# A hybrid decoder step on one core: the samples' value rows go to all partitions by DMA through scratch memory, not by products with a selecting matrix

## The chip, the cores and the metric

The kernel runs on one core of a Trainium2 chip. A core has a matrix engine (TensorE, PE in the rows), VectorE (DVE), ScalarE (ACT), GpSimd (POOL) and SyncE (SP), and 16 DMA engines that serve transfers issued from SP and from GpSimd. The metric is the device time of one execution, in microseconds (us), as the median of several runs.

## The reference

A two-layer decoder trunk is computed for 256 prompt tokens and for 8 samples of one new token each. Layer 0 mixes by pooling, layer 1 by gated linear attention (GLA); each is followed by an MLP, and all four blocks by a layer norm. The change lies in the state update of the GLA layer for the samples. Cut to that:

```python
q, k, v, og, gk_low = jnp.split(x @ w_in, ...)          # 4 heads, DK = 256, DV = 512
log_a = log_sigmoid(gk_low @ w_gate_up + gate_bias) / 16
# per token: S_t = diag(a_t) S_{t-1} + k_t^T v_t ;  o_t = q_t S_t
S_new = S * exp(b_last) + einsum('bhjk,bhjv->bhkv', k, v)
o = einsum('bhik,bhkv->bhiv', q * exp(bcum), S) + ...
```

For a sample there is one token, so for each sample and head the 256 x 512 state is scaled row by row by `a`, the outer product of the sample's key (256 numbers) and value row (512 numbers) is added, the new state is written out, and it is multiplied with the query.

## The kernel before

**Layout.** Activations lie transposed: features on the 128 partitions, and 264 columns (256 prompt tokens, then the 8 samples). Weights are read in units of 128 x 2048. `stage()` issues a unit's load from SP and splits each half in two parts, `whi` (a cast on ScalarE, L134) and `wlo` (a subtraction on VectorE, L135); `project()` makes 16 x 3 products of a unit (L147 to L149) into a bank `ps`. Six halves, three units, are held, and a unit is staged two units ahead of its use.

**Order.** TensorE's program is in the order in which the code is written; the other engines' programs are ordered by a scheduler. `project()` calls `slot()` after every 12 products. A `slot()` runs what `later()` has put off, and moves each background chain on to its next `yield`. So one `yield` in a chain is a slot of 12 products, and all side work of GLA stands between such slots. The chains are `main_chain` (prompt attention, head after head), `sample_chain` (the samples, head after head) and `rms_chain`.

**Values.** `Head.value(t, ...)` is called for each of the four 128-feature tiles of a head's values. Some slots later its `turn()` transposes the tile on TensorE against `ident` into a bank `ma` (there are two such banks): two transposes for the prompt (L509, copied by L513 to `vtok`), and a third for the samples (L510, from `vp`, the samples' 8 columns as two parts, copied by L514 to `vs`).

**Samples.** `Head.samples()` handles 8 samples in two rounds of four. `load(b)` brings both halves of a sample's state from memory on SP's queue into `s0`, which has nine buffers for the eight halves of a round; `decay(b)` scales it on ScalarE (L612). Per sample, TensorE multiplies `vs` by a column of `pick` that is repeated 128 times; this leaves the sample's 512-value row on all partitions of the bank `mc` (L629). VectorE then adds key times row to each half of the state (L632), and GpSimd issues its store (L633). Two more yields and the next sample follows; after four of them come eight products of states and queries (L643). Buffers of `s0` come free when these products and the stores have read them. At the end of a head the result is transposed (L657).

**Prompt.** In `Head.chain()` the score products of a level (L474) are copied from `ma` under a mask (L478); after the attention products (L528) the keys are turned (L565) and copied to `ktok` (L566), and two slots or so later the new prompt state is made from it (L572) and stored by GpSimd (L575).

Of the kernel before, what the change touches and what calls it, by code (L numbers as in the profile page):

```python
# [6 lines left out]
F32 = mybir.dt.float32  # L7
F32R = mybir.dt.float32r
U8 = mybir.dt.uint8
AF = mybir.ActivationFunctionType  # L10
ALU = mybir.AluOpType
PSUM = bass.MemoryType.PSUM

P = 128
D = 2048
KT = D // P
NP = 256
NS = 8
# [7 lines left out]
DV = 512  # L26
# [20 lines left out]
def hybrid_step(tc, a, o, stop=None):  # L47
    nc = tc.nc
    with ExitStack() as ctx, tc.manual_schedule(engines={mybir.EngineType.PE}):
        _body(ctx, tc, nc, a, o, stop)  # L50


def _body(ctx, tc, nc, a, o, stop):
    V, S, PE, G = nc.vector, nc.scalar, nc.tensor, nc.gpsimd
# [5 lines left out]
    work = pool("work", 6)  # L60
# [3 lines left out]
    def wtile():  # L64
        return work.tile([P, N], F32, name="wt")

    def bank(tag):
        return misc.tile([P, 512], F32, name=tag, bufs=2 if tag == "ma" else 1)
# [3 lines left out]
    ident = keep.tile([P, P], F32, name="ident")  # L72
# [11 lines left out]
    def hslot(s, i, shape, dt, name):  # L84
        return hp.tile(shape, dt, name=name, tag=f"{s}{i}")
# [78 lines left out]
    def later(n, fn):  # L164
        pending.append([n, fn])

    def project(x, ncol=N):
        w = next_unit()
        ps = acc.tile([P, NX], F32, name="ps")
        for k in range(KT):  # L170
            c = slice((k % 8) * P, (k % 8 + 1) * P)
            hi, lo = w[k // 8]
            mm3(ps[:, :ncol], hi[:, c], lo[:, c], x.hi[k][:, :ncol], x.lo[k][:, :ncol], k == 0, k == KT - 1)
            if k % 4 == 3:
                slot()
        return ps
# [186 lines left out]
    def gla(gctx, norm, xp, x, hg):  # L363
        gp = gctx.enter_context(tc.tile_pool(name="gp", bufs=1))
# [21 lines left out]
        wg = gp.tile([P, KT * 32], F32, name="wg", tag="st", bufs=2)  # L386
        low = gp.tile([P, N], F32, name="low", tag="st", bufs=2)
        nc.sync.dma_start(wg, a["wgk"])
        pick = gp.tile([P, NS], F32R, name="pick")
        G.memset(pick.bitcast(F32), 0.0)  # L390
        G.tensor_tensor(pick[:2 * NS], ident[:2 * NS, :NS], ident[:2 * NS, NS:2 * NS], op=ALU.add)

# [34 lines left out]
        class Head:  # L429
# [64 lines left out]
            def value(self, t, ps, raw):  # L494
                v = wtile()
                evacuate(v, ps, raw)

                vp = work.tile([P, 2 * NS], F32R, name="vp", bufs=4)
                V.tensor_copy(vp[:, :NS], v[:, NP:])
                V.tensor_tensor(vp[:, NS:], v[:, NP:], vp[:, :NS].bitcast(F32), op=ALU.subtract)  # L500

                def turn():
                    if t == 0:
                        self.vtok = [hslot(hg, 8 + 2 * self.h + b, [P, DV], F32, "vtok") for b in range(2)]
                        self.vs = hslot(hg, self.h % 2, [P, DV], F32R, "vs")
                        V.memset(self.vs.bitcast(F32), 0.0)
                    tp = bank("ma")
                    for b in range(2):
                        PE.transpose(tp[:, b * P:b * P + P], v[:, b * P:b * P + P], ident)  # L509
                    PE.transpose(tp[:2 * NS, NP:NP + P], vp.bitcast(F32), ident)  # L510
                    c = slice(t * P, t * P + P)
                    for b in range(2):
                        V.tensor_copy(self.vtok[b][:, c], tp[:, b * P:b * P + P])  # L513
                    S.copy(self.vs[:2 * NS, c], tp[:2 * NS, NP:NP + P])  # L514
                    self.turned = t + 1

                if not raw:
                    later(2, turn)
                else:
                    self.turns = getattr(self, "turns", []) + [turn]  # L520
                    if t == 3:
                        for e, fn in enumerate(self.turns):
                            later(2 + e, fn)
# [77 lines left out]
            def samples(self):  # L601
                h = self.h
                s0s = {}

                def load(b):
                    s0s[b] = [half("s0") for _ in range(2)]
                    for hf in range(2):
                        nc.sync.dma_start(s0s[b][hf], a["st"][h, b][:, hf])

                def decay(b):  # L610
                    for hf in range(2):
                        S.mul(s0s[b][hf], s0s[b][hf], sa[:, 2 * h + hf, b:b + 1])  # L612

                for b in range(4):
                    load(b)
                while self.turned < 4:
                    yield
                for r in range(2):
                    V.tensor_copy(qpad[:, :, 4 * r:4 * r + 4, r], self.q[:, :, NP + 4 * r:NP + 4 * r + 4])
                decay(0)  # L620
                yield
                op = bank("mb")
                for r in range(2):
                    if r:
                        decay(4)
                        yield
                    for b in range(4 * r, 4 * r + 4):
                        vb = bank("mc")
                        PE.matmul(vb, lhsT=pick[:, b:b + 1].broadcast_to([P, P]), rhs=self.vs, start=True, stop=True)  # L629
                        for hf in range(2):  # L630
                            s0 = s0s[b][hf]
                            V.scalar_tensor_tensor(s0, vb, self.k[:, hf, NP + b:NP + b + 1], s0, ALU.mult, ALU.add)  # L632
                            nc.gpsimd.dma_start(o["ngs"][h, b][:, hf], s0)  # L633
                        yield
                        if b % 4 < 3:
                            decay(b + 1)
                            yield
                            yield
                    yield
                    for hf in range(2):  # L640
                        for c in range(4):
                            b = 4 * r + c
                            PE.matmul(op[32 * c:32 * c + 32], lhsT=qpad[:, hf, b], rhs=s0s[b][hf],  # L643
                                      start=r == 0 and hf == 0, stop=r == 1 and hf == 1, tile_position=(0, 32 * c))
                        yield
                    if r == 0:
                        for b in range(4, NS):
                            load(b)
                        yield
                        yield  # L650
                os_ = gp.tile([P, DV], F32, name="os", tag="st", bufs=2)
                S.copy(os_, op)
                yield
                yield
                tp = bank("ma")
                for t in range(4):
                    PE.transpose(tp[:, t * P:t * P + P], os_[:, t * P:t * P + P], ident)  # L657
                tv = tp.rearrange("p (t c r) -> p t r c", t=4, c=4)
                V.tensor_copy(self.oT[:, :, NP:].rearrange("p t (r c) -> p t r c", r=2), tv[:, :, :2])
                self.sampled = True  # L660
# [32 lines left out]
        def evacuate(dst, ps, raw, scale=1.0):  # L693
            if raw:
                t, col = settle(ps)
                V.tensor_scalar(dst, t, col, scale, ALU.subtract, ALU.mult)
            else:
                S.mul(dst, ps[:, :N], scale)

        heads = []  # L700
        gated = Parts(hg, ())
# [39 lines left out]
    with tc.tile_pool(name="poolp", bufs=2) as pp:  # L741
# [68 lines left out]
        ln = Norm("mix_0", xs, 0, half=True, first=4)  # L810
# [20 lines left out]
    ln = mlp(0, ln, xs, Parts("b"), lambda: Parts("a"))  # L831
# [2 lines left out]

    with ExitStack() as gctx:
        xr = Parts("b")
        gated = gla(gctx, ln, ln.x, xr, "a")
        for m in range(KT):
            S.mul(Z[m], xr.hi[m][:, :N].bitcast(F32), ALPHA)
            V.scalar_tensor_tensor(Z[m], xr.lo[m][:, :N].bitcast(F32), ALPHA, Z[m], ALU.mult, ALU.add)  # L840
        xs = Parts("b")
        tc.keep_in_program_order(S.preload_act_table(AF.Abs_reciprocal_sqrt))
        ln = Norm("mix_1", xs)
        for m in range(KT):
            ln.add(project(gated))
    if stop == "gla":
        return dump(ln)
    ln = mlp(1, ln, xs, Parts("a"), None)
# [94 lines left out]
```

## Time and profile before

| what | value |
|---|---|
| median of 3 runs | 2057.54 us (2055.9 to 2058.04) |
| the profiled execution's own time | 2056.8 us |
| its span from first to last instruction | 2055.0 us |
| granted TensorE clock, mean | 0.993 of full |
| TensorE busy | 2022.8 us, 98% of the span |
| VectorE, ScalarE, GpSimd busy | 61%, 52%, 3% |

The span is 1.8 us shorter than the execution's own time. Matmuls are pipelined, so each shows a duration that overlaps the next one's; what a matmul costs is read from start to start. GpSimd's row for a transfer is the time it takes to issue it, and "to landing" is from issue until the data have arrived. GLA's side work lies between about 866 and 1170 us.

### The profile page before, as it was taken

The numbers are of one execution on the slowest core, as the hardware profiler recorded it, in microseconds if no ns is written. First come the engines' busy times: TensorE is split into PE (matmuls) and PEld (weight loads), VectorE is DVE, ScalarE is ACT, GpSimd is POOL, SyncE is SP. The second block draws the span as 40 slices with busy tenths as digits, with TensorE's granted clock in tenths as the row PEclk, the third lists the DMA queues.
The fourth block names the chain that finished last, engine by engine and source line by source line (L and its number), as shares of the span: only waits on it lengthen the run. The fifth ranks groups of instructions, "written<-read, shape, count | busy, mean of one in ns | idle before, by whom it ended". The sixth has DMA issues, their size and how long they took to land.

```text
span 2055.0 us, 38509 instructions
## 1 busy us (share of the span) xinstructions
PE 2022.8 (98%) x16308; PEld 1985.2 (97%) x16308; DVE 1255.5 (61%) x1983; ACT 1077.8 (52%) x1618; POOL 54.8 (3%) x129
## 2 busy tenths in 40 slices
PE   8899999999999999999999999999999999999996
PEld 7899999999999999998899999999999999999996
DVE  6866455444444568986778768866445444445465
ACT  4457355345435545856666645566454345435543
POOL 0000000000000000011111010000000000000000
PEclk9999999999999999999999999999999999999998
DMA  7555555555555554477676455545555555555552
GB/s 293 182 183 185 185 180 178 178 184 184 185 175 177 182 185 168 160 257 258 244 264 235 165 177 174 180 170 183 185 185 182 178 176 183 185 181 179 178 180 84
DMA packets 66877, 387.76 MB, mean 189 GB/s; under 512 B 7856, under 2 KB 10672, under 8 KB 25216
## 3 DMA queue, kind: packets, MB, share of 16 engines
q1 hardware_dynamic: 60816, 366.01, 51.3%
q0 software_dynamic: 5888, 19.30, 2.5%
q8 instruction: 127, 2.08, 0.4%
q14 instruction: 46, 0.38, 0.1%
HBM read 364.24 MB, written 22.14 MB: 188 GB/s over the span
## 4 chain that ended last, share of the span: by engine, by line
PE 94%; DVE 4%; DMA 1%; ACT 1%; issue 0%; SPq 0%; ACTq 0%; POOL 0%; DVEq 0%
PE ps L147 30%; PE ps L148 30%; PE ps L149 30%; PE ma L474 1%; PE mb L643 1%; PE ma L572 1%; DVE wlo L135 1%; PE ps L792 0%; PE mc L629 0%; DMA pw<-in_pw 0%; DVE zt L302 0%; PE ma L528 0%; DMA s<-in_st 0%; DVE zt L303 0%; DMA raw<-in_w 0%
## 5 line engine op out<-in xcount | busy, mean ns | idle before, releaser
L148 PE MATMUL ps<-hl,whi 128*128 128x264 f32 (+1 forms) x5120 | 1455.7, 284 | 0.0
L147 PE MATMUL ps<-hh,whi 128*128 128x264 f32 (+1 forms) x5056 | 1449.4, 287 | 4.5 <-ACT whi L134 4.5
L149 PE MATMUL ps<-hh,wlo 128*128 128x264 f32 (+1 forms) x5056 | 1436.1, 284 | 3.4 <-DVE wlo L135 3.4
L135 DVE TENSOR_TENSOR wlo<-raw,whi 128x1024 fp32r<-128x1024 f32 x640 | 783.6, 1225 | 594.8 <-ACT whi L134 592.2
L134 ACT CAST whi<-raw 128x1024 fp32r<-128x1024 f32 x640 | 671.4, 1051 | 840.6 <-PE ps L148 806.0
L147 PEld LDWEIGHTS ps<-hh,whi 128*128 128x128 f32 x5056 | 952.7, 188 | 21.3 <-issue 15.8
L148 PEld LDWEIGHTS ps<-hl,whi 128*128 128x128 f32 x5120 | 965.2, 189 | 3.7 <-issue 1.4
L149 PEld LDWEIGHTS ps<-hh,wlo 128*128 128x128 f32 x5056 | 952.8, 188 | 3.7 <-DVE wlo L135 3.7
L180 DVE TENSOR_TENSOR hl<-wt,hh 128x264 fp32r<-128x264 f32 x188 | 80.0, 432 | 17.6 <-ACT hh L179 11.7
L179 ACT CAST hh<-wt 128x264 fp32r<-128x264 f32 x188 | 76.9, 412 | 7.5 <-DVE wt L666 3.3
L355 DVE TENSOR_TENSOR zt<-zt,ps 128x264 f32<-128x264 f32 x96 | 41.2, 429 | 61.6 <-PE ps L149 61.5
L341 ACT ACTIVATE wt<-wt 128x264 f32<-128x264 f32 x128 | 54.6, 427 | 4.0
L632 DVE SCALAR_TENSOR_TENSOR s<-mc,k,s 128x512 f32<-128x512 f32 x64 | 45.8, 746 | 3.0 <-PE mc L629 3.0
L340 ACT ACTIVATE wt<-ps,par 128x264 f32<-128x264 f32 x96 | 45.7, 476 | 0.0
L612 ACT ACTIVATE s<-s,sa 128x512 f32<-128x512 f32 x64 | 43.0, 718 | 3.4 <-DMA s<-in_st 3.3
L633 POOL DMA_DIRECT2D out_ngs<-s x64 | 34.7, 542 | 348.3 <-DVE s L632 340.5
L213 DVE SCALAR_TENSOR_TENSOR zt<-ps,zt 128x264 f32<-128x264 f32 x48 | 20.8, 434 | 35.5 <-PE ps L149 35.5
L792 PE MATMUL ps<-px,pw 128*128 128x264 f32 x128 | 31.9, 403 | 3.7 <-DMA pw<-in_pw 3.7
L255 ACT ACTIVATE wt<-zt 128x264 f32<-128x264 f32 x60 | 23.7, 412 | 16.8 <-DVE zt L213 16.7
L792 PEld LDWEIGHTS ps<-px,pw 128*128 128x128 f32 x128 | 24.7, 199 | 8.1 <-issue 3.8
L248 ACT ACTIVATE hh<-zt,par 128x264 fp32r<-128x264 f32 x48 | 24.4, 512 | 12.5 <-DVE zt L213 8.8
L304 ACT ACTIVATE wt<-zt,par 128x264 f32<-128x264 f32 x48 | 27.6, 604 | 1.1 <-DVE zt L303 1.1
(178 smaller groups left out, 851.7 us busy)
## 6 DMA issues: line engine op xcount, KB each, us to landing
raw<-in_w SPq DMA_DIRECT2D x256, 1024.0 KB, 4.8
raw<-in_win SPq DMA_DIRECT2D x48, 1024.0 KB, 5.3
s<-in_st SPq DMA_DIRECT2D x64, 256.0 KB, 5.6
out_ngs<-s POOLq DMA_DIRECT2D x64, 256.0 KB, 3.2
raw<-in_wout SPq DMA_DIRECT2D x16, 1024.0 KB, 4.8
pw<-in_pw SPq DMA_DIRECT2D x4, 1024.0 KB, 8.8
zt<-in_xf SPq DMA_DIRECT2D x4, 528.0 KB, 9.4
out_y<-zt SPq DMA_DIRECT2D x8, 264.0 KB, 2.2
```

What stands on the lines that cost most here:

```text
L134: S.copy(hi, src)
L135: V.tensor_tensor(lo, src, hi.bitcast(F32), op=ALU.subtract)
L147: PE.matmul(ps, lhsT=whi, rhs=xh, start=start, stop=False)
L148: PE.matmul(ps, lhsT=whi, rhs=xl, start=False, stop=False)
L149: PE.matmul(ps, lhsT=wlo, rhs=xh, start=False, stop=stop_)
L179: S.copy(x.hi[m][:, :N], src)
L180: V.tensor_tensor(x.lo[m][:, :N], src, x.hi[m][:, :N].bitcast(F32), op=ALU.subtract)
L340: S.activation(t, project(x)[:, :N], AF.Relu, bias=bias)
L341: S.activation(t, t, AF.Square)
L612: S.mul(s0s[b][hf], s0s[b][hf], sa[:, 2 * h + hf, b:b + 1])
L632: V.scalar_tensor_tensor(s0, vb, self.k[:, hf, NP + b:NP + b + 1], s0, ALU.mult, ALU.add)
L792: PE.matmul(ps[:, :N], lhsT=w[:, c], rhs=px[2 * g + k // 2][:, k % 2], start=k == 0, stop=k == 3)
```

## The change

The three-part transposing and the products with `pick` go. The samples' columns of the four value tiles are gathered in one tile `vp`; after the fourth turn a single transpose makes 32 rows of 128 from it, ScalarE copies them to `vs`, and GpSimd stores them to a scratch tensor `vd` in device memory, ordered by sample. For each sample `spread(b)` then reads its 512-value row from there, repeated for all 128 partitions, into `vb`, which has two buffers (`hslot` 0 and 1). The first two spreads are issued at the head's start; each further one is issued when both halves of the sample two before it have been updated, and ahead of that sample's two stores. The head's first update comes two slots later than it did. GpSimd's program, in GLA only, is in source order.

```diff
-        pick = gp.tile([P, NS], F32R, name="pick")
-        G.memset(pick.bitcast(F32), 0.0)
-        G.tensor_tensor(pick[:2 * NS], ident[:2 * NS, :NS], ident[:2 * NS, NS:2 * NS], op=ALU.add)
+        dram = gctx.enter_context(tc.tile_pool(name="dram", bufs=2, space=bass.MemoryType.DRAM))
...
-                vp = work.tile([P, 2 * NS], F32R, name="vp", bufs=4)
-                V.tensor_copy(vp[:, :NS], v[:, NP:])
-                V.tensor_tensor(vp[:, NS:], v[:, NP:], vp[:, :NS].bitcast(F32), op=ALU.subtract)
+                if t == 0:
+                    self.vp = work.tile([P, 4, NS], F32, name="vp", bufs=2)
+                V.tensor_copy(self.vp[:, t], v[:, NP:])
...
-                        self.vs = hslot(hg, self.h % 2, [P, DV], F32R, "vs")
-                        V.memset(self.vs.bitcast(F32), 0.0)
...
-                    PE.transpose(tp[:2 * NS, NP:NP + P], vp.bitcast(F32), ident)
...
-                    S.copy(self.vs[:2 * NS, c], tp[:2 * NS, NP:NP + P])
+                    if t == 3:
+                        tp = bank("ma")
+                        PE.transpose(tp[:4 * NS, :P], self.vp.rearrange("p t b -> p (t b)"), ident)
+                        vs = gp.tile([4 * NS, P], F32, name="vs")
+                        S.copy(vs, tp[:4 * NS, :P])
+                        self.vd = dram.tile([NS, 4, P], F32, name="vd")
+                        nc.gpsimd.dma_start(self.vd.rearrange("b t c -> t b c"), vs)
...
+                def spread(b):
+                    vb[b] = hslot(hg, b % 2, [P, DV], F32, "vb")
+                    nc.gpsimd.dma_start(vb[b], self.vd[b:b + 1].rearrange("b t c -> b (t c)").broadcast_to([P, DV]))
...
+                spread(0)
+                spread(1)
                 decay(0)
+                yield
+                yield
                 yield
...
-                        vb = bank("mc")
-                        PE.matmul(vb, lhsT=pick[:, b:b + 1].broadcast_to([P, P]), rhs=self.vs, start=True, stop=True)
                         for hf in range(2):
                             s0 = s0s[b][hf]
-                            V.scalar_tensor_tensor(s0, vb, self.k[:, hf, NP + b:NP + b + 1], s0, ALU.mult, ALU.add)
-                            nc.gpsimd.dma_start(o["ngs"][h, b][:, hf], s0)
+                            V.scalar_tensor_tensor(s0, vb[b], self.k[:, hf, NP + b:NP + b + 1], s0, ALU.mult, ALU.add)
+                        if b + 2 < NS:
+                            spread(b + 2)
+                        for hf in range(2):
+                            nc.gpsimd.dma_start(o["ngs"][h, b][:, hf], s0s[b][hf])
...
-        gated = gla(gctx, ln, ln.x, xr, "a")
+        with tc.manual_schedule(engines={mybir.EngineType.Pool}):
+            gated = gla(gctx, ln, ln.x, xr, "a")
```

In the changed program the lines are some numbers off: the update is L640, the spread L617, the store of a half L644, the new transpose L511, the keys' copy L567.

On TensorE, around the second sample of head 0, this stood (`mc` the bank with the row, `ps` a weight unit's bank):

```order
L148 MATMUL ps<-hl,whi 128x264
L149 MATMUL ps<-hh,wlo 128x264
L629 MATMUL mc<-vs,pick 128x512
L147 MATMUL ps<-hh,whi 128x264
L148 MATMUL ps<-hl,whi 128x264
```

At the same place L147 now follows L149 at once, and at the end of the head's turns stands the one transpose for the samples:

```order
L149 MATMUL ps<-hh,wlo 128x264
L505 MATMUL ma<-ident,wt 128x128 x2
L511 MATMUL ma<-ident,vp 32x128
L147 MATMUL ps<-hh,whi 128x264
L148 MATMUL ps<-hl,whi 128x264
```

So 32 products and 16 transposes leave TensorE's program and four transposes enter it.

On GpSimd, at the start of head 0's samples, the program now reads (`out_ngs` is the output of the states; before, its stores alone stood here, two per sample):

```order
L515 DMA vd<-vs 4x8x128
L617 DMA vb<-vd 128x512 x3
L644 DMA out_ngs<-s_9332 128x512
L644 DMA out_ngs<-s_9333 128x512
L617 DMA vb<-vd 128x512
L644 DMA out_ngs<-s_9336 128x512
L644 DMA out_ngs<-s_9337 128x512
L617 DMA vb<-vd 128x512
```

The spread of sample 2 stands ahead of the stores of sample 0, and so on.

On VectorE, at the change from head 1 to head 2, this stood where the turned keys of head 1 are copied (`s_11279` and `s_11280` are the second sample of head 2):

```order
L585 TENSOR_TENSOR wt<-wt 128x264
L566 COPY ktok<-ma 128x512
L464 TENSOR_TENSOR kt_8828<-k,kt_8828 128x64x4
L451 TENSOR_TENSOR suf<-suf,zt 128x64x4
L452 TENSOR_TENSOR zt<-zt 128x2x32x4
L592 TENSOR_SCALAR wt<-ma 128x264
L632 SCALAR_TENSOR_TENSOR s_11279<-mc,k,s_11279 128x512
L632 SCALAR_TENSOR_TENSOR s_11280<-mc,k,s_11280 128x512
```

and now, with `s_11318` to `s_11323` the first two samples of head 2:

```order
L625 COPY qpad<-q 128x2x4
L640 SCALAR_TENSOR_TENSOR s_11318<-vb,k,s_11318 128x512
L640 SCALAR_TENSOR_TENSOR s_11319<-vb,k,s_11319 128x512
L640 SCALAR_TENSOR_TENSOR s_11322<-vb,k,s_11322 128x512
L640 SCALAR_TENSOR_TENSOR s_11323<-vb,k,s_11323 128x512
L135 TENSOR_TENSOR wlo<-raw,whi 128x1024
L567 COPY ktok<-ma 128x512
```

The updates no longer follow a product of TensorE, and two samples' updates have moved ahead of the keys' copy.

## Rows read from the trace of the kernel before

**Rows 1.** The page, busy time of each engine.

```profile
PE 2022.8 (98%) x16308; PEld 1985.2 (97%) x16308; DVE 1255.5 (61%) x1983; ACT 1077.8 (52%) x1618; POOL 54.8 (3%) x129
```

**Rows 2.** Busy time by stretch; granted clock, DMA share and rate come last.

```profile
core 0: us, PE busy (x) PEld busy (x) DVE busy (x) ACT busy (x) POOL busy (x), PEclk, DMA share, GB/s
866.00:1131.00 265.00, 264.14 (x2064) 241.54 (x2067) 206.59 (x449) 162.34 (x287) 37.89 (x70) 1.00 0.71 248
1190.00:1500.00 310.00, 309.99 (x2531) 309.45 (x2531) 206.20 (x338) 170.04 (x253) 3.52 (x11) 1.00 0.52 180
```

**Rows 3.** Waits of TensorE from 840 to 1180: engine, line, releaser, total, times, longest.

```profile
PE ma L657 <- ACT vs L514: 0.7, 1, 0.7
```

**Rows 4.** Timeline of TensorE around two pick products of head 0: start, duration.

```profile
878.39 0.28 PE L149 MATMUL ps<-hh,wlo 128*128 128x264 f32 x1
878.50 0.40 PE L629 MATMUL mc<-vs,pick 128*128 128x512 f32 x1
878.74 0.28 PE L147 MATMUL ps<-hh,whi 128*128 128x264 f32 x1
878.86 0.28 PE L148 MATMUL ps<-hl,whi 128*128 128x264 f32 x1
...
883.99 0.40 PE L629 MATMUL mc<-vs,pick 128*128 128x512 f32 x1
```

**Rows 5.** Timeline of TensorE at the first two turns of head 0.

```profile
866.08 0.38 PE L509 MATMUL ma<-ident,wt 128*128 128x128 f32 x2
866.30 0.27 PE L510 MATMUL ma<-ident,vp 128*16 128x128 f32 x1
866.40 0.38 PE L509 MATMUL ma<-ident,wt 128*128 128x128 f32 x2
```

**Rows 6.** Lines L629 and L510: count, shortest, median, longest in ns.

```profile
L629 PE MATMUL mc<-vs,pick x32: 390/474/791, 872.9 to 1127.6; 128*128 128x512 f32 x32
L510 PE MATMUL ma<-ident,vp x16: 272/272/278, 866.3 to 1072.9; 128*16 128x128 f32 x16
```

**Rows 7.** Groups of VectorE and ScalarE, 860 to 1180: busy, mean ns, idle before.

```profile
L135 DVE TENSOR_TENSOR wlo<-raw,whi 128x1024 fp32r<-128x1024 f32 x79 | 96.6, 1223 | 30.2 <-ACT whi L134 29.8
L632 DVE SCALAR_TENSOR_TENSOR s<-mc,k,s 128x512 f32<-128x512 f32 x64 | 45.8, 746 | 3.0 <-PE mc L629 3.0
L552 DVE TENSOR_TENSOR kt<-k,kt 128x512 f32<-128x512 f32 x4 | 2.8, 689 | 0.0
L134 ACT CAST whi<-raw 128x1024 fp32r<-128x1024 f32 x79 | 82.8, 1048 | 72.5 <-PE ps L148 62.3 <-issue 4.9 <-ACT kt L463 1.8
```

**Rows 8.** Transfers: KB each, median us to landing; spread of L608; GpSimd's issue time.

```profile
out_ngp<-st POOLq DMA_DIRECT2D x8, 256.0 KB, 2.3
mf<-in_masks POOLq DMA_DIRECT2D x1, 224.0 KB, 3.7
out_npp<-in_xtail POOLq DMA_DIRECT2D x1, 120.0 KB, 3.7
DMA to landing us min/median/max: 2.9/5.6/7.4
L633 POOL DMA_DIRECT2D out_ngs<-s x64: 539/542/562, 874.7 to 1130.5; - x64
```

**Rows 9.** Timelines of TensorE, ScalarE and VectorE: last turn and first sample, head 0.

```profile
870.54 0.27 PE L510 MATMUL ma<-ident,vp 128*16 128x128 f32 x1
871.94 0.26 ACT L514 CAST vs<-ma 16x128 fp32r<-16x128 f32 x1 [0.20 <-DVE vtok L513]
873.63 1.42 DVE L632 SCALAR_TENSOR_TENSOR s<-mc,k,s 128x512 f32<-128x512 f32 x2
875.74 0.45 DVE L478 COPY_PREDICATED at<-masks,ma 128x64 f32<-128x64 uint8 x2 [0.36 <-PE ma L474]
```

**Rows 10.** Timelines of TensorE and VectorE: turning head 1's keys.

```profile
1011.04 0.49 PE L565 MATMUL ma<-ident,kt 128*128 128x128 f32 x3
1012.04 0.68 DVE L566 COPY ktok<-ma 128x512 f32<-128x512 f32 x1
```

More of the change, by code (lines that the diff above doesn't have):

```diff
@@ L612, in decay @@
                         S.mul(s0s[b][hf], s0s[b][hf], sa[:, 2 * h + hf, b:b + 1])
+                def spread(b):
+                    vb[b] = hslot(hg, b % 2, [P, DV], F32, "vb")
+                    nc.gpsimd.dma_start(vb[b], self.vd[b:b + 1].rearrange("b t c -> b (t c)").broadcast_to([P, DV]))
+                vb = {}
                 for b in range(4):
```

## The prediction

> **What bounds the kernel now.** I read the page's busy times first: TensorE is busy for 98% of the span [rows 1], so the other engines matter only where they make it wait. A matmul's busy time overlaps its neighbour's, so I then looked at the stretch of the change for idle time. From 866 to 1131 us, where all samples are handled, TensorE shows 264.14 of 265 us busy at a granted clock of 1.00, VectorE 206.59, and the DMA engines 71% at 248 GB/s; afterwards they move 180 [rows 2]. The reader should see that TensorE has no room there and VectorE has about a fifth. The waits of TensorE confirm it: from 840 to 1180 us there is one, 0.7 us, on the copying of the samples' values [rows 3]. So what the change takes out of TensorE's program is time won one for one, unless it puts a wait back.
>
> **The change part by part.** *The pick products.* A regular product follows the one before it after 0.12 us (878.74 to 878.86), and across a pick product the regular ones stand 0.35 us apart (878.39 to 878.74) [rows 4]. So a pick product costs 0.23 us, although its own row says a median of 474 ns [rows 6]. There are 32: 32 x 0.23 = 7.4 us. From the product's start to the next it is 0.24 us, which would be 7.7; if a part of its fill were hidden in the others, 0.21, it would be 6.7.
>
> The Trainium skill, "TensorE: Matmul & The Clock Gate", section "Back-to-back issue gap", gives some 131 ns per product as sustained for 512 columns in a stream with weight loads, against 216 ns for an isolated one. By the first figure 32 products are an estimated 4.2 us and the sum at the end of this part 5.0, by the second 6.9 and 7.7; the trace's 0.23 us agrees with the second and decides.
>
> *The transposes.* Two prompt transposes take 0.22 us to the next start, and the samples' one 0.10 [rows 5]. Sixteen go (1.6 us) and four come, one per head. The new one has 32 weight columns for 16 and the same 128 moving columns, so I take 0.11: 0.4 us. Together -1.2 us.
>
> *Waits that go with them.* The one wait of 0.7 us was for the old copy to `vs` [rows 3]. The new transposing takes a bank `ma` of its own behind the turn's, which can make the next user of `ma` wait as long. I set the two against each other at 0.
>
> *The update.* The row now comes from SBUF. It took 746 ns with the row in a bank of PSUM, where TensorE writes; an operation of VectorE on as many columns with both inputs in SBUF takes 689 [rows 7]. That is 64 x 57 ns = 3.6 us off VectorE, not off TensorE; a value above 746 is not excluded, but 64 x 0.1 us more would still fit in its 58 idle us of 265 [rows 2].
>
> *The spreads.* Each is 256 KB on all partitions, 32 in all, 8.4 MB: over 265 us some 32 GB/s on top of 248 [rows 2]. No row shows a repeated read of one line. The nearest are GpSimd's load of 224 KB, 3.7 us to landing, and SyncE's loads of 256 KB in the busy stretch, 2.9 to 7.4, median 5.6 [rows 8]. I take 3.8 and keep 2.3 (a store of the same size) to 7.4. GpSimd needs 0.54 us to issue one [rows 8], in order: the spread of sample b+2 waits for both updates of b, and b's stores stand behind it and so land 0.6 us later. Nobody waits at once for these stores but the loads of the next round, and those wait for the products of the round as well.
>
> Is it covered? From one sample to the next it is 5.49 us now (878.50 to 883.99 [rows 4]) and 0.23 less without the product, so two samples take 10.5 us. A buffer `vb` goes round in two updates (1.4 us) and a landing, 1.4 + 3.8 = 5.2 us, or 8.8 at 7.4. Both are under 10.5; the point from which it decides is a landing of 9.1 us.
>
> *The start of a head.* In head 0 nothing is ahead: the last turn is at 870.54, the copy to `vs` ends 1.7 us later (871.94 + 0.26), the store to scratch lands 2.3 to 3.7 us after that [rows 8, 9], and the first spread 3.8 later: 878.3 to 879.7. VectorE did the first update at 873.63 and the next masked copy at 875.74 [rows 9]. With two more yields (24 products, 2.9 us) and with that masked copy and a weight split now ahead of it, it will come to the update at about 877.5, and then stands for 1 to 2 us, at a landing of 7.4 for about 5. Behind it are the second sample, a weight split and masked copies. Each of these has room: weights are staged two units ahead, a unit is 48 x 0.12 = 5.8 us, and a half costs 1.05 us on ScalarE and 1.22 on VectorE, so some 9 of 11.6 us are spare, which the ScalarE row shows as 62.3 us of waiting for TensorE to release weights [rows 7]. The masked copies have three slots from one to the next. For heads 1 to 3 the scratch row is written while the head before is finishing. So no TensorE time.
>
> *The free updates.* An update used to wait for a product of TensorE, which held it in its place. Now the scheduler has moved some forward, and ahead of the keys' copy of head 1 stand four updates and a weight split. The copy began 1.0 us after the transposes and took 0.68 [rows 10]; the product that needs it follows some two slots, 2.9 us, after the transposes. If the states arrive just as the keys do, 4 x 0.69 + 1.22 + 0.68 = 4.7 us stand there, 1.8 too many; at a load of 7.4 instead of 5.6 us, 3.6. If they come earlier it is 0. By the code the loads start some three slots and their side products ahead, so that the end is near 0: I count 0 to 1 us, once, and take 0.4.
>
> *Sum.* 7.4 + 1.2 - 0.4 = 8.2 us off the profiled execution's 2056.8 us: 2048.6. The median of the runs is 0.7 us above that execution, so in medians it is 2049.3; I put 2048.8. A difference of 0.2%, 4.1 us, is about what a measurement of this kernel can tell from no change.
>
> **The rivals.** *Part given back.* Updates that stand early in VectorE's program wait for rows or states there, and copies out of `ma` behind them come late, at some of the seven places where a head begins after another (three) or a round's states are loaded anew (four): 0.6 to 1.5 us at three of them, or 0.25 to 0.65 at all, 1.7 to 4.6 us. For it: two `ma` banks only, and the four updates above. Against it: a fifth of VectorE's time is idle and the side products are three slots apart. 2050.5 to 2053.5.
>
> *Not faster: all of it given back.* The same with 0.7 to 1.7 us at all seven, or with the 3.6 us above at each of the three head changes: 4.7 to 12 us, 2053.5 to 2061.
>
> *A short pick product.* If the pick products' time is mostly refilled by the stream around them, at 0.13 us each: 32 x 0.13 + 1.2 - 0.4 = 5.0, so 2051.8. The time between the regular products on both sides speaks against it [rows 4], so I give it little.
>
> The Trainium skill's first figure above is of that kind.
>
> *Slower: a slow repeated read.* All 128 descriptors of a spread read the same 2 KB. If that lands after 12 us, each pair of samples takes 13.4 us for 10.5, and with 16 pairs VectorE, and TensorE behind it at the state products, loses 46 us less 8.2: 2095. From a landing of about 9.9 us (16 x 0.8 = 13) it is slower than before. Against it: no transfer of this size in the rows is above 7.4.
>
> The Trainium skill, "DMA: Bandwidth & Descriptors", section "Latency and other measured facts", reports half the rate where rows lie at large powers of two apart, and supposes that such streams meet in one memory channel. No run here shows a read of that kind yet.
>
> **How the numbers follow.** The forecast has 0.64 (2046.5 to 2050.5; the lower end has 7.7 us for the products, the 0.7 us wait gone and no late copy, 2047.4, and 0.9 for the runs' own spread), part given back 0.14, the short product 0.03, all given back 0.11, slower 0.08. The range of 8 in 10 takes the forecast, the part given back and the short product: 2046.5 to 2053.5. Faster by more than 0.2% is 0.64 + 0.14 + 0.03 = 0.81, within it 0.11, slower 0.08.
>
> **What would show it.** Regular products should follow one another at 0.12 us where the pick products stood, and the stretch of GLA should be some 8 us shorter, with the rest of the program unchanged. Spreads should land in 2.3 to 7.4 us; updates should take about 0.69 us. VectorE may wait for a spread, longest at head 0's first update. TensorE's waits from 840 to 1180 us should stay near 1 us. The prediction is wrong if TensorE waits there for copies to `ktok` or `vtok`, for masked copies or for updated states with more than some 3 us together, or if a spread lands after more than 9 us.

## The result: slower, and the profile after

| | us (runs) |
|---|---|
| before | 2056.94 (5 runs, 2055.9 to 2058.04) |
| after | 2070.31 (5 runs, 2063.56 to 2073.14) |
| ratio | 1.0058, 95% interval 1.0047 to 1.0070 |

The changed kernel is 0.58% slower where 0.4% faster was forecast, and its runs lie 9.6 us apart where those of before lie 2.1 apart. The profiled execution is its fastest, 2063.56 us, span 2061.8; the median lies 6.8 us above it, and no trace shows where these went (mean granted clock 0.991 in the profiled execution, 0.989 to 0.992 in the others). Stretches of it as in [rows 2], and four of 10 us:

```profile
866.00:1131.00 265.00, 253.66 (x1949) 229.31 (x1949) 192.74 (x407) 151.45 (x262) 53.45 (x99) 0.98 0.78 266
910.00:920.00 10.00, 10.00 (x73) 10.00 (x72) 9.61 (x20) 4.99 (x8) 2.16 (x4) 0.83 0.86 304
1000.00:1010.00 10.00, 8.23 (x46) 4.88 (x47) 3.85 (x8) 4.18 (x9) 1.73 (x3) 0.83 0.70 225
1010.00:1020.00 10.00, 7.84 (x57) 7.12 (x56) 5.67 (x10) 6.66 (x11) 0.00 (x0) 0.96 0.63 188
1020.00:1030.00 10.00, 10.00 (x54) 7.42 (x53) 5.43 (x11) 7.76 (x14) 3.88 (x8) 0.87 0.58 194
1190.00:1500.00 310.00, 310.00 (x2530) 309.45 (x2530) 207.59 (x342) 169.33 (x252) 5.91 (x16) 1.00 0.52 179
```

TensorE, busy for 264.14 of these 265 us before, now idles for 11.3, and close behind some of the idle times its granted clock falls: 0.83 is a mean over 10 us between its levels of 1.2 and 2.4 GHz. If each short window lost what its mean lacks, that is an estimated 1.7 + 1.7 + 0.4 + 1.3 = 5.1 us. So 10.5 us of new idle time and 5.1 of slow clock less the forecast 8.2 us make 7.4; the profiled executions differ by 6.8. Part of this agreement is chance. The 2001st product of L149 starts at 792.0 us before and at 790.1 after, the 3001st at 1283.5 and 1290.3, so the stretch around GLA is 8.7 us longer, and 1.3 of them are not accounted for. Behind the samples (1190 to 1500) nothing has changed.

TensorE's waits from 840 to 1180 us (as [rows 3]), and below them VectorE's for the updates' inputs:

```profile
PE ma L505 <- ACT wt L709: 2.4, 2, 1.4
PE ma L573 <- DVE ktok L567: 2.2, 1, 2.2
PE ma L472 <- DVE at L490: 1.8, 1, 1.8
PE ma L472 <- DVE at L476: 1.6, 1, 1.6
PE ma L668 <- ACT zt L531: 1.1, 1, 1.1
```

```profile
DVE s L640 <- DMA vb<-vd: 23.6, 11, 5.0
DVE s L640 <- ACT s L613: 6.9, 5, 2.9
DVE s L640 <- DMA out_ngs<-s: 5.7, 1, 5.7
DVE s L640 <- issue: 4.1, 1, 4.1
```

None of TensorE's waits is for a row or a state. All are for `ma` (three shorter ones, 2.2 us together, are left out): copies, masks and evacuations, that is copies out of a bank, that stand in VectorE's or ScalarE's queue. VectorE stands 23.6 us waiting for rows, in 11 places. Two more are for rows by their times: the 5.7 us that the view puts down to a store and the 4.1 that it puts down to nothing ("issue") end at 1033.84 and 1062.41, as the rows spread from 1027.20 and 1055.45 land. That makes 33.4 us in 13 places.

By what stood ahead in the queue, 5.5 of TensorE's 11.3 us come right behind an update that had waited for its row (masks at L490 and L476, `ktok`). Another 3.5 (L709, L531) are evacuations on ScalarE, behind decays and casts that had waited for states and raw weights, and 1.9 are the new transpose's. Head 2's start shows how the one becomes the other: GpSimd, VectorE, TensorE (`vd` is the scratch memory, `out_ngp` the prompt's state).

```profile
1003.78 0.64 POOL L515 DMA_DIRECT2D vd<-vs  x1 [10.22 <-ACT vs L513]
1008.77 1.09 POOL L617 DMA_DIRECT2D vb<-vd  x2 [4.35 <-DMA vd<-vs]
1023.53 0.54 POOL L576 DMA_DIRECT2D out_ngp<-st  x1 [13.68 <-ACT st L575]
1027.20 0.54 POOL L617 DMA_DIRECT2D vb<-vd  x1
```

```profile
1009.30 0.18 DVE L625 COPY qpad<-q 128x8 f32<-128x8 f32 x1 [4.71 <-PE mb L654]
1013.96 1.42 DVE L640 SCALAR_TENSOR_TENSOR s<-vb,k,s 128x512 f32<-128x512 f32 x2 [4.48 <-DMA vb<-vd]
1015.71 1.42 DVE L640 SCALAR_TENSOR_TENSOR s<-vb,k,s 128x512 f32<-128x512 f32 x2 [0.33 <-DMA vb<-vd]
1017.04 1.22 DVE L135 TENSOR_TENSOR wlo<-raw,whi 128x1024 fp32r<-128x1024 f32 x1
1018.17 0.69 DVE L567 COPY ktok<-ma 128x512 f32<-128x512 f32 x1
```

```profile
1018.91 2.66 PE L573 MATMUL ma<-vtok,ktok 128*128 128x512 f32 x3 [2.16 <-DVE ktok L567]
```

The scratch store is issued at 1003.78; GpSimd waits 4.35 us for it to land, and the first rows are there at 1013.96, 10.2 us after the store. VectorE has stood at the first update since 1009.48, with the keys' copy five instructions behind, and TensorE waits for that copy. After two spreads GpSimd stands 13.7 us at the store of the prompt's state, which is next in source order, so the third spread goes out at 1027.20. From store to first update it is 7.2 us in head 0 and 13.6, 10.2 and 9.6 in heads 1 to 3.

Landings (page, KB and median) and the spread's three values:

```profile
s<-in_st SPq DMA_DIRECT2D x64, 256.0 KB, 5.6
out_ngs<-s POOLq DMA_DIRECT2D x64, 256.0 KB, 5.9
vb<-vd POOLq DMA_DIRECT2D x32, 256.0 KB, 5.4
...
DMA to landing us min/median/max: 3.4/5.4/7.4
```

### The profile page after: what moved, and what is told of

Its sections match the earlier page's. It is cut to its first block, busy times and chain, and to the rows that moved or that the text cites. A ratio compares the mean times of both kernels' runs of the same rounds, so it can differ in the third digit from the quotient of the medians.

```text
span 2061.8 us, 38434 instructions
## 1 busy us (share of the span) xinstructions
PE 2019.9 (98%) x16264; PEld 1980.9 (96%) x16264; DVE 1249.8 (61%) x1963; ACT 1071.8 (52%) x1606; POOL 73.6 (4%) x163
## 4 chain that ended last, share of the span: by engine, by line
PE 90%; DMA 3%; DVE 3%; issue 2%; ACT 1%; POOL 0%; SPq 0%; ACTq 0%; POOLq 0%; DVEq 0%
PE ps L147 29%; PE ps L148 29%; PE ps L149 29%; DMA s<-in_st 1%; PE ma L472 1%; DMA vb<-vd 1%; PE ma L573 1%; DVE wlo L135 0%; PE mb L654 0%; PE ps L803 0%; DMA raw<-in_win 0%; DMA pw<-in_pw 0%; ACT s L613 0%; ACT whi L134 0%; DVE zt L302 0%
## 5 line engine op out<-in xcount | busy, mean ns | idle before, releaser
L147 PE MATMUL ps<-hh,whi 128*128 128x264 f32 (+1 forms) x5056 | 1452.2, 287 | 4.9 <-ACT whi L134 4.9
L149 PE MATMUL ps<-hh,wlo 128*128 128x264 f32 (+1 forms) x5056 | 1437.0, 284 | 3.4 <-DVE wlo L135 3.4
L147 PEld LDWEIGHTS ps<-hh,whi 128*128 128x128 f32 x5056 | 953.6, 189 | 22.1 <-issue 14.6
L149 PEld LDWEIGHTS ps<-hh,wlo 128*128 128x128 f32 x5056 | 953.5, 189 | 3.7 <-DVE wlo L135 3.7
L640 DVE SCALAR_TENSOR_TENSOR s<-vb,k,s 128x512 f32<-128x512 f32 x64 | 47.3, 750 | 40.4 <-DMA vb<-vd 23.6
L613 ACT ACTIVATE s<-s,sa 128x512 f32<-128x512 f32 x64 | 43.9, 717 | 21.3 <-DMA s<-in_st 21.2
L644 POOL DMA_DIRECT2D out_ngs<-s x64 | 34.4, 540 | 23.9 <-DVE s L640 16.8
L207 POOL CAST hh<-par 128x4 fp32r<-128x4 f32 x24 | 5.2, 233 | 685.0 <-PE ps L149 675.3
L803 PEld LDWEIGHTS ps<-px,pw 128*128 128x128 f32 x128 | 23.5, 190 | 6.3 <-DVE px L785 2.7
```

The source lines that it names most:

```text
L147: PE.matmul(ps, lhsT=whi, rhs=xh, start=start, stop=False)
L149: PE.matmul(ps, lhsT=wlo, rhs=xh, start=False, stop=stop_)
L640: V.scalar_tensor_tensor(s0, vb[b], self.k[:, hf, NP + b:NP + b + 1], s0, ALU.mult, ALU.add)
L803: PE.matmul(ps[:, :N], lhsT=w[:, c], rhs=px[2 * g + k // 2][:, k % 2], start=k == 0, stop=k == 3)
```

## The experiments

Theory A: updates wait for rows in VectorE's queue and hold up the copies behind them. Theory B: the transfers' load on the DMA engines delays state loads, weights and stores. Others came up on the way: C, the turn of the state buffers; D, the order that the scheduler set; E, any update that is held late; F, the prompt's stores in GpSimd's queue. Each kernel was timed next to the kernel before, 4 to 11 times:

| run | us | ratio (95% interval) |
|---|---|---|
| x1_still | 2050.04 | 0.9962 (0.9948 to 0.9975) |
| x2_unread | 2052.73 | 0.9979 (0.9970 to 0.9988) |
| x9_unread_order_after | 2051.65 | 0.9977 (0.9969 to 0.9986) |
| x15_unread_anchored | 2055.55 | 0.9996 (0.9987 to 1.0005) |
| x4_anchored | 2062.33 | 1.0022 (1.0013 to 1.0031) |
| x11_before_pool | 2056.57 | 0.9999 (0.9991 to 1.0008) |
| x8_before_plus_pool | 2071.30 | 1.0079 (1.0066 to 1.0092) |
| x3_before_plus | 2084.74 | 1.0130 (1.0116 to 1.0143) |
| x5_rows4 | 2066.97 | 1.0053 (1.0040 to 1.0066) |
| x7_early_rows | 2066.11 | 1.0050 (1.0037 to 1.0062) |
| x17_rows4_early | 2066.88 | 1.0053 (1.0041 to 1.0066) |
| x6_rows4_anchored | 2065.09 | 1.0044 (1.0030 to 1.0058) |
| x12_state5 | 2069.97 | 1.0061 (1.0047 to 1.0074) |
| x13_state5_anchored | 2061.33 | 1.0018 (1.0009 to 1.0027) |
| x18_rows4_slack | 2061.40 | 1.0025 (1.0015 to 1.0035) |
| x19_slack | 2079.03 | 1.0112 (1.0098 to 1.0126) |
| x21_ngp_act | 2076.50 | 1.0100 (1.0085 to 1.0116) |
| x22_rows4_ngp_act | 2069.33 | 1.0061 (1.0048 to 1.0074) |

**Rows not moved, moved but unread, and unread in the changed kernel's order.** The updates read `ones` in all three; x1 also drops the store and the spreads.

```diff
-V.scalar_tensor_tensor(s0, vb[b], self.k[...], s0, ALU.mult, ALU.add)
+V.scalar_tensor_tensor(s4, ones.unsqueeze(1).broadcast_to([P, 4, P]), self.k[...], s4, ALU.mult, ALU.add)
```

> Of the change, no row moves: neither the 16 KB store nor the 32 spreads is issued, and the updates read a tile of ones (so the state outputs are not the kernel's). The pick products are gone as in the changed kernel (2070.3). All theories that put the loss on rows (their waits in VectorE's queue, or the load they put on the DMA engines) expect the forecast gain here: 2048 to 2051. If the loss lies in the order alone (updates that stand freely in VectorE's queue, GpSimd in source order), it stays at 2060 or more. If the removed products were worth less than 8 us, it is 2053 to 2057.

> Store and all 32 spreads are issued as in the changed kernel, but nobody reads the rows: the updates read a tile of ones (state outputs are not the kernel's). Theory A, waits: the updates stand in VectorE's queue waiting for rows and hold up the copies behind them; without those waits 2048 to 2053. Theory B, load: the spreads' 8.4 MB and their bursts hold up state loads, raw weights and stores whoever reads them; it stays at 2062 to 2070.

x1 gives the forecast gain: 0.38% is 7.8 us (5.1 to 10.7). The same transfers without a reader take back 0.17% of it, 3.5 us, hardly more than the noise (the intervals overlap). But without waits the scheduler had also set another order, so x9 adds the changed kernel's order, 417 instructions of VectorE and 227 of ScalarE:

```diff
+ORDER = {"DVE": "...", "Activation": "..."}
...
+    for row in ORDER.values():
+        for first, second in zip(row, row[1:]):
+            tc.add_manual_dep(traced[second], first, edge, reason="order")
```

> The kernel with unread rows (updates read ones, state outputs not the kernel's; 2052.7), but with VectorE's and ScalarE's instructions held to the very order in which they stand in the changed kernel, row for row. All four queues are then the changed kernel's; only the waits for rows are missing. Theory A, waits for rows: 2050 to 2055. Theory D, order: the scheduler set the changed kernel's order for rows that it took to land later or earlier than they do, and this order itself is slow: 2062 to 2070.

Theory A holds, and the order by itself is harmless: all instructions of the kernel's text stand where the changed kernel has them, and only the rows' readers are gone (with them the spreads' wait for updates that have read the tile): 0.9977 for 1.0058, 0.81% or 16.7 us. Its stretch, all waits of TensorE from 840 to 1180 us, and waits of VectorE and ScalarE:

```profile
866.00:1131.00 265.00, 260.54 (x2043) 239.33 (x2043) 205.84 (x434) 160.13 (x280) 55.41 (x102) 0.99 0.79 278
```

```profile
PE ma L510 <- ACT wt L715: 1.3, 1, 1.3
PE ma L534 <- ACT zt L536: 1.2, 1, 1.2
PE ma L516 <- DVE vtok L513: 0.9, 1, 0.9
PE ma L674 <- ACT zt L536: 0.6, 1, 0.6
PE ma L534 <- DVE vtok L513: 0.5, 1, 0.5
```

```profile
DVE s L646 <- ACT s L618: 11.3, 7, 3.8
...
ACT s L618 <- DMA s<-in_st: 22.1, 15, 4.9
ACT whi L139 <- DMA raw<-in_win: 15.7, 8, 3.5
```

The DMA engines are as loaded as in the changed kernel, and ScalarE waits as long for states and raw weights (there 21.2 and 16.5 us), yet TensorE idles for 4.5 us only: 3.1 for ScalarE's evacuations, 1.4 for copies to `vtok`, none for a mask or `ktok`.

**Updates held behind their slot**, with rows read (x4) and unread (x15):

```diff
+last = next(i for i in reversed(nc.cur_bb.bb.instructions) if i.engine == mybir.EngineType.PE)
-V.scalar_tensor_tensor(s0, vb[b], ...)
+u = V.scalar_tensor_tensor(s0, vb[b], ...)
+tc.add_manual_dep(u.ins, last.name, mybir.DependencyInfo(mybir.DependencyClass.NoSync, ...), reason="slot")
```

> The changed kernel; each update is held in VectorE's queue behind the slot in which it is written in the source (an ordering edge to the last TensorE instruction issued before it, no wait in the hardware). Same transfers, same queues. Theory A with the place of the updates as cause (the scheduler put them up to several instructions ahead, where they wait for rows): most of the loss goes, 2050 to 2058. Theory B, load: no change, 2062 to 2072.

> Unread rows (updates read ones; state outputs not the kernel's), each update held behind its slot. In the changed kernel's own order unread rows gave 2051.7, and held updates with read rows 2062.3. Theory A, waits for rows alone: 2050 to 2055. Theory E, any late update: under the transfers' load the state loads come late, and an update that may not use the first free moment after its decay (held for a slot, for a pick product or for a row) pushes the lateness on; then 2060 to 2067 without a single wait for a row.

Holding the updates gives back 0.36%, 7.4 us, of the loss, and VectorE's row waits fall from 33.4 to 3.9 us. The profiled executions show little of this gain: their spans differ by 2.3 us, and TensorE idles as long as in the changed kernel. x4's stretch and two of its waits:

```profile
866.00:1131.00 265.00, 253.70 (x1972) 232.07 (x1972) 194.50 (x411) 151.89 (x263) 52.09 (x96) 0.99 0.78 268
...
PE ma L670 <- ACT zt L531: 4.0, 1, 4.0
PE ma L472 <- DVE at L490: 2.7, 1, 2.7
```

The 2.7 us follow the longest row wait that is left, 2.8 us at head 1's first update, whose spread had stood behind the stores of the prompt's state until 946.25. The 4.0 us are an evacuation behind decays that waited for states. Reading rows still costs 0.26% in this order, and holding alone, without a reader, 0.19% (x15 less x9), each known to about 0.13%. So here theories A and E cannot be told apart in size; of the whole loss, 0.81% by x9, theory A has the larger part.

**Transfers added to the kernel before.** GpSimd in source order alone (x11), with 32 unread transfers (x8), and these in the scheduler's order (x3):

```diff
+                def spread(b):
+                    row = hslot(hg, (14, 14, 8, 10)[h] + b % 2, [P, DV], F32, "row")
+                    nc.gpsimd.dma_start(row, a["st"][h, b][0:1, 0].broadcast_to([P, DV]))
...
+        with tc.manual_schedule(engines={mybir.EngineType.Pool}):
+            gated = gla(gctx, ln, ln.x, xr, "a")
```

> The kernel before, pick products and all, with 32 further transfers of GpSimd that each repeat one row of 2 KB over 128 partitions (read from the states' memory, into tiles that nobody reads), at the places of the spreads. Theory A, waits: 2056 to 2059, since nothing waits for them but POOL. Theory B, load: what the change lost (some 13 us net and 8 of gain eaten, 21 in all) appears here too: 2067 to 2078.

> The kernel before with nothing but GpSimd held to source order (it moves stores of the prompt's state only). Control for the run of before with unread transfers in source order (2071.3). If the order of GpSimd is harmless: 2055 to 2058, and the 15 us of that run are the transfers'. If it isn't: 2062 or more.

> The kernel before with the 32 unread transfers once more, now with GpSimd held to source order (in the earlier run of that kind, 2084.7, the free order had put eight of them ahead of the first store). If the load of the transfers is worth what the run with unread rows showed (2.7 us), 2058 to 2062. If that run was slow through the place of the stores behind them, all of the 27 us goes with the order; if through the load that they put on the kernel before, with its busier VectorE slots, it stays above 2070.

GpSimd's source order costs nothing. In x3 the scheduler put eight transfers ahead of the first store, and TensorE waited 15.0 us in three places for ScalarE's evacuation of values. In x8 that is gone, but 0.8%, 16 us, stays, where 2058 to 2062 was expected of a light load. ScalarE waits no longer than in x9 (states 18.3 us, weights 10.0); its state loads land later (median 7.5 us for 5.9). Nobody reads a row there, and the loss goes through ScalarE's queue: copies that TensorE needs stand behind decays whose states are late. Head 2 in x8 (ScalarE, TensorE):

```profile
1012.32 1.40 ACT L616 ACTIVATE s<-s,sa 128x512 f32<-128x512 f32 x2 [3.08 <-DMA s<-in_st]
1013.63 0.35 ACT L530 COPY zt<-ma 128x256 f32<-128x256 f32 x1
```

```profile
1014.03 0.70 PE L528 MATMUL ma<-at,vtok 128*128 128x256 f32 x2 [2.19 <-ACT zt L530]
```

Four waits of this kind (1.5, 2.2, 1.9 and 1.7) are 7.3 of TensorE's 11.1 idle us. Why the states come later there, and why the kernel before bears this load so much worse than the changed one, is not settled; no run separates its 16 copies to `vs` from the updates' tie to TensorE's products.

**More lead, an earlier source, both, and both cures with held updates.** Four row tiles (x5), spreads that read the states' memory (x7), both (x17), four tiles and held updates (x6):

```diff
-vb[b] = hslot(hg, b % 2, [P, DV], F32, "vb")
+vb[b] = hslot(hg, (b % 4 if b % 4 < 2 else (14, 14, 8, 10)[h] + b % 4 - 2), [P, DV], F32, "vb")
-                        if b + 2 < NS:
+                        if b + 4 < NS:
...
-nc.gpsimd.dma_start(vb[b], self.vd[b:b + 1].rearrange("b t c -> b (t c)").broadcast_to([P, DV]))
+nc.gpsimd.dma_start(vb[b], a["st"][h, b][0:1, 0].broadcast_to([P, DV]))
```

> The changed kernel with four row tiles in place of two (the two more lie in slots of other heads that are idle then), so that a spread is issued three to four samples ahead of its reader, not one to two. Theory A1, too short a lead: the updates find their rows landed, and what is left is the load (2.7 us in the run with unread rows) and the first rows of a head: 2051 to 2056. Theory A2, the first rows of each head, which go through the store and back, cost most of it: 2060 to 2068, since these are as late as before. Theory B, load: 2065 to 2072.

> The changed kernel, but the spreads read rows of the states' memory, which is there from the start, in place of the stored value rows (state outputs are not the kernel's); the store is still made, nobody waits for it. Theory A2, the way through scratch memory (store 4.3 us, then the spread) at each head's start: most of the loss goes, 2052 to 2058. Theory A1, two tiles give too short a lead throughout: a small part goes, 2062 to 2069. Theory B, load: none goes.

> Four row tiles, and spreads that read memory which is there from the start (state outputs not the kernel's): the lead of three to four samples and no way through scratch memory, each of which alone gave 4 us back at most (2067.0 and 2066.1). Theory A: no wait for a row is left, and so 2051 to 2056. If it stays at 2062 or more, waits for rows don't explain the loss by themselves.

> Four row tiles, and each update held behind its slot as well. The anchor alone gave back 8 of the 13 us, and if lead and place are two halves of one cause (updates that stand ahead of their rows), both together give 2050 to 2054, no better than the rows that nobody reads (2052.7) by more than 2. If the place alone matters it stays at 2058 to 2063.

None of the four gives back more than 0.14%. x17 misses theory A's 2051 to 2056 clearly; VectorE still waits for rows, 15.5 us in five places, the longest this:

```profile
1033.19 0.75 DVE L640 SCALAR_TENSOR_TENSOR s<-vb,k,s 128x512 f32<-128x512 f32 x1 [6.28 <-DMA vb<-in_st]
```

and GpSimd had stood at the stores of the prompt's state until 1025.45, with the spreads behind them leaving from 1026.00 on. In x6 VectorE's row waits are down to 5.2 us, but the longest, 3.8 us at head 1's first update, stands ahead of a mask for which TensorE waits in turn:

```profile
PE ma L472 <- DVE at L490: 4.1, 1, 4.1
```

GpSimd had stood at the stores of the prompt's state until 946.62, and the spreads left from 947.15 on. ScalarE waits 26.0 us for states and 23.5 for raw weights in x6. That four spreads at once compete with these loads (theory B) is not shown: x5 issues the same four, and ScalarE waits 16.4 and 17.5 there.

**A fifth state tile** (x12), and with held updates (x13): theory C, the turn of the state buffers.

```diff
+                    if b == 4:
+                        s0s[b] = [hslot(hg, (14, 14, 8, 10)[h] + hf, [P, DV], F32, "s4") for hf in range(2)]
...
+                load(4)
```

> The changed kernel with two more state tiles (idle slots of other heads), so that the fifth sample's state is loaded with the first four and does not wait for a buffer to turn (update, store, readout, load). Theory C, the turn of the state buffers is the loop that got longer (stores land in 5.9 us in place of 3.2, updates come late, so loads, decays and all that stands behind them in ScalarE's queue are late): a third to two thirds of the loss goes, 2056 to 2063. Theory A, waits for rows only: 2066 to 2072.

> The same with each update held behind its slot. Theory C: below the anchored kernel (2062.3) by 4 or more, 2050 to 2058. If it gives back nothing beyond the anchor, 2060 to 2064, and the turn of the buffers is not what is left there.

Theory C gets no support: neither differs from its kernel without the tile (1.0058 and 1.0022). In x12 ScalarE waits 38.7 us for states (21.2 in the changed kernel), so the earlier load brought the states no earlier.

**Slack**, with four row tiles (x18) and with two (x19): three more yields before a head's first update, two after the second loads. x18 also has head 3's extra row tiles in another idle slot.

```diff
-                yield
-                yield
-                yield
+                for _ in range(6):
+                    yield
                 op = bank("mb")
```

> The changed kernel, real rows, with four row tiles, three more yields (4.1 us of TensorE's time) between a head's first spreads and its first update, and two more between the loads of the second four states and their decay. TensorE's work is the same; heads of samples end later, which nothing waits for until the gates of the same head. Theory A: rows are there when the updates come, 2050 to 2056, ahead of the kernel before. Theory E: the slack helps the loads too, the same. If load alone sets the loss, 2062 or more.

> The same slack with the changed kernel's two row tiles. Theory A: the first rows of each head come in time, those behind them not (two tiles): 2058 to 2066. If the slack alone does it (2050 to 2056), the loss was at the heads' starts and at the turn of the states, and the third and fourth tile matter little.

With four tiles it helps (1.0025 for 1.0053), with two it harms. In x19 VectorE waits 36.4 us for rows, and TensorE's longest waits, 4.9 us twice, are for the sums of the norm (`wt` L586), which stand between and behind updates that wait.

**The prompt's state out of GpSimd's queue** (theory F):

```diff
-nc.gpsimd.dma_start(o["ngp"][self.h, hf], st)
+nc.scalar.dma_start(o["ngp"][self.h, hf], st)
```

> The changed kernel, real rows, two row tiles; the eight stores of the prompt's state are issued by ScalarE, which writes their tile, and no longer stand in GpSimd's queue. Theory F: in source order these stores stand ahead of spreads and wait for ScalarE's copy (13.7 us in head 2, 17.2 in head 3 of the profiled run), so the rows behind them are 5 to 15 us late, and that is the larger part of the row waits: 2055 to 2063. Theory A1, two tiles are too short a lead even so: 2064 to 2070.

> The same with four row tiles. Theory F with A1: with nothing in front of the spreads and a lead of three to four samples, rows are there when their update comes, and what unread rows gave comes with real ones: 2051 to 2056, no slower than the kernel before. If it stays above 2062, GpSimd's queue is not what makes the rows late.

Theory F falls as a cure: x21 is slower than the changed kernel, and x22 no faster; VectorE waits 39.4 and 20.0 us for rows. Head 1 in x21 (GpSimd, VectorE, TensorE):

```profile
937.26 0.64 POOL L515 DMA_DIRECT2D vd<-vs  x1 [17.97 <-ACT vs L513]
944.43 1.09 POOL L617 DMA_DIRECT2D vb<-vd  x2 [6.53 <-DMA vd<-vs]
```

```profile
947.93 2.08 DVE L640 SCALAR_TENSOR_TENSOR s<-vb,k,s 128x512 f32<-128x512 f32 x3 [8.75 <-DMA vb<-vd]
949.92 0.18 DVE L670 COPY zt<-ma 128x32 f32<-128x32 f32 x1
```

```profile
950.16 2.07 PE L488 MATMUL ma<-q,k 128*128 128x128 f32 x8 [2.47 <-DVE zt L670]
955.67 0.81 PE L590 MATMUL ma<-wt,ones 128*128 128x264 f32 x1 [3.43 <-DVE wt L586]
```

The queue is free, but the store's landing alone holds the spreads until 944.43 (945.63 in the changed kernel). VectorE reaches the first update at 939.2, where it reached it at 948.3 in the changed kernel, and stands 8.75 us with the copies behind it. Here a freer GpSimd brought the spread 1.2 us earlier, and VectorE came to the update 9.1 us earlier.

No version that reads the rows beats the kernel before; the nearest are x13, x4 and x18.

## Why the prediction was wrong, step by step

*The products and transposes: right.* Regular products follow one another at 0.12 us where the pick products stood (877.76, 877.88, 878.00), and x1 gives 7.8 us where 8.2 were forecast. Of the Trainium skill's two figures ("TensorE: Matmul & The Clock Gate", section "Back-to-back issue gap"), the sum by the sustained one, 5.0, lies just outside the run's interval, that by the isolated one inside. "I set the two against each other at 0" was a small miss: the new transpose waits 0.93 us each in heads 0 and 2, for its bank and for `vp`.

*The update: wrong, without effect.* It takes 741 to 764 ns, not 689: with both inputs from SBUF no faster than with one from PSUM [rows 7]. x9's updates take as long (744 to 754), and it is fast.

*The spreads: right in the bounds.* They land in 3.4 to 7.4 us, median 5.4, where 3.8 was taken; no step of the sum hung on that, and the slow repeated read did not come. 128 reads of one row land as fast as a state of the same size, 5.6 us. The Trainium skill's halved rate ("DMA: Bandwidth & Descriptors", section "Latency and other measured facts") is for rows at large powers of two apart; one row read again and again is another pattern, and no run here bears on that figure. Their load costs 0.15 to 0.17% in the changed kernel's frame (x9, x2 less x1).

*"Is it covered?": failed in part.* The ring of two tiles was set against two samples' time, as if a spread left when its tile was free. Between them lies GpSimd's queue in source order, with 13.7 us at the prompt's state in head 2.

*The start of a head: right for head 0, failed for the others.* VectorE came to head 0's first update at 875.52 (forecast about 877.5) and stood 1.58 us (1 to 2), until the row was there at 877.10 (878.3 to 879.7). But "for heads 1 to 3 the scratch row is written while the head before is finishing. So no TensorE time" is wrong: store to row took 9.6 to 13.6 us there, and VectorE stood 1.72, 4.48 and 4.99 us at the first updates.

*The free updates: the step that decided it.* It saw the mechanism (updates no longer held in their place, ahead of the keys' copy), and 2.16 us at that copy lie in its 0 to 3.6. But its term counted one place, 0.4 us, and waits for states only. Rows were waited for in 13 places; new idle time of TensorE is 10.5 us, and the granted clock, in no term of the sum, costs an estimated 5.1 more in the profiled execution. The sign that the prediction had named came: TensorE waits 5.6 us for masked copies and `ktok`, where more than 3 was to show it wrong. x9 shows the size by itself: 16.7 us for the same queues with and without a reader.

*The rivals.* "All of it given back" (0.11) had the right mechanism and ended at 2061. Even the profiled execution lies 2.5 us beyond, less than the 5.1 that the clock, which was not in its prices, cost there. The room that was held against it (a fifth of VectorE's time, 9 us of weights) is an average: an in-order queue that stands at one row gives none of it to the copy behind.

*Open:* why unread transfers cost the kernel before 16 us and the changed one 3.5; where the 6.8 us between the profiled execution and the median lie; and how lead, source, queue and load share what x5 to x7, x17 and x22 leave, since each of these edits also moved the scheduler's order, which only x9 held fixed.

## What to carry to other kernels

When a product on a busy engine is replaced by a transfer, price the whole way to the data (store, landing, issue, landing: here 7 to 14 us, not one landing of 5), and list what stands behind the reader in its in-order queue. To part the load of a transfer from the wait for it, leave the data unread and hold the order of every queue. A scheduler that may move the reader can undo a cure for the late row by placing the reader earlier, as in x21's head 1. ScalarE's queue showed the same: in x8 no row is read, and late states hold up its copies in just this way.

## Not expected of the hardware

A store of 16 KB to scratch memory took 3.2, 4.2 and 6.8 us to land (least, median, most), hardly less than transfers 16 times its size. TensorE's granted clock fell after waits as short as 1 to 2 us: to means of 0.83 behind one of 1.4 us (910 to 920 us) and around two of 1.0 and 0.9 (1000 to 1010), and to 0.96 and 0.87 behind one of 2.2 (1010 to 1030). It stayed at 1.00 around waits of 1.8 us (950 to 960) and 1.6 (1060 to 1070). The changed kernel's runs lie 0.46% apart for 0.1% before, x5's 0.41% and x13's 0.48%; but x12 and x17, whose updates wait for rows as well, have 0.15% and 0.13%, so what sets this spread is not shown.
